# Second up phase of a decoder step: another order of five products, an earlier load, one copy replaced

## The chip, the cores and the metric

The kernel runs on one core of a Trainium2 chip. The metric is device time in microseconds, the median of three runs. TensorE (PE) multiplies; VectorE (DVE) and ScalarE (ACT) prepare its weights and read its results out of PSUM; SyncE (SP) issues nearly all loads and stores; GpSimd (POOL) does little.

## The reference

One layer of a decoder serves a prompt of 512 tokens and 8 samples of 4 tokens, 544 columns in all, in float32. It consists of a combined input projection, a pooling mixer, a sparse attention, an output projection, and a ConvFFN. The change lies in the ConvFFN:

```python
up = rmsnorm(h, g_pre_ffn) @ w_up            # 2048 -> 2 x 5632
val, gate = jnp.split(up, 2, axis=-1)
gcat = jnp.concatenate([conv_hist, gate], axis=1)
conv = conv_b
for j in range(CONV_WIDTH):                  # three taps along the tokens
    conv = conv + conv_w[j] * gcat[:, j:j + T]
y = (jax.nn.gelu(conv, approximate=True) * val) @ w_down
h = h + rmsnorm(y, g_post_ffn)
```

## The kernel before

**Layout.** Activations lie with channels on the 128 partitions and the 544 tokens in two halves of 272 (H2). Every product of float32 numbers is made of three matmuls: high part by high part, low part of the activations by high part of the weights, and high by low (lines 354, 355 and 356). So each block of weights is split first: ScalarE casts it to its high part (wh, line 232), and VectorE subtracts that to get the low part (wl, line 234). `Weights` walks through a list of units that `plan()` writes; a unit here is 8 blocks of 128x128, 512 KB, multiplied with 272 columns in 24 matmuls. While one unit is multiplied, the unit two places further is split (line 254, with `ahead` 2): its cast is issued after the first of 8 blocks, its low part after the sixth. Before a unit begins, `get()` runs the functions that were hooked to its number (line 248).

**The up projection in two phases.** It is done for 44 column tiles j (FT) in a scheme of the Strassen-Winograd kind on 2x2 blocks: half the channels by half the tokens on one side, the value and gate tiles by half the channels on the other. The first phase multiplies with the plain first half of the tokens and leaves in `stash_d`, in DRAM, 128x544 numbers for each j: in one half a partial sum, in the other the finished gate with its activation. The second phase, which the change touches, runs one group for each j with five products, whose activations are the prepared forms t2, t1, t3, t4 and b22. Their weights are four sums of quarters of `w_up` and one plain quarter (3):

- s1 = q2 + q3, s2 = s1 - q0, s3 = q0 - q2, s4 = q1 - s2, each a 128x1024 operation on VectorE (line 1338). `give()` hooks the loads of the quarters (line 206, called by `quarter`) and these sums to units before the one that uses them.

**One group.** A group has two PSUM banks, `ug` (`pa`) and `utr` (`ph`), each with two buffers that take turns between groups. An identity matmul first puts the stash's first half (`sl`) into ug (line 1487); then t2 is added to ug, t1 starts utr, t3 is added to ug, t4 to ug, and b22 to utr. In between the results are read: u2 is ug after t2 (ScalarE, line 1489), u3 is ug after t3 (ScalarE, line 1492), val is u3 + utr after t1 (VectorE, line 1493), act is the stash's second half times ug after t4 (line 1495), and ge, the gate, is u2 + utr after b22 (lines 1500 and 1501). `conv()` then hangs the three taps, the GELU and the product with val on a clock that ticks with the blocks of the units (`later`). act and val go to `act_d` in DRAM (lines 1496 and 1443), from where the down phase loads them.

**What sets the order.** All engines work in program order, and the program is the order in which this code is written. SP's queue is in that order too: a load that waits holds up those behind it. `prefetch(j + 1)` loads the next stash (line 1415) and copies two edges into the next ge; before the change it stands behind the store of act.

Of the kernel before, what the change touches and what calls it, by code (L numbers as in the profile page):

```python
# [12 lines left out]
F32 = mybir.dt.float32  # L13
# [3 lines left out]
OP = mybir.AluOpType  # L17
# [4 lines left out]
P = 128  # L22
# [5 lines left out]
TOK = SEQ + NB * NS  # L28
H2 = TOK // 2
# [5 lines left out]
FT = DFF // P  # L35
# [16 lines left out]
def kinner(mat, m, kts=None, halves=BOTH):  # L52
    kts = list(range(KT) if kts is None else kts)
    return [(tuple((mat, k, m) for k in kts[i:i + 8]), halves) for i in range(0, len(kts), 8)]


def kouter(mat, ms):
    return [(tuple((mat, k + i, m) for i in range(2) for m in ms), BOTH) for k in range(0, KT, 2)]


def grp(gs):
    return [(tuple(("grp%d" % g, k, m) for g in gs for m in range(2) for k in range(2)), BOTH)]


def plan():
    u = kouter("in", [0, 1, 2])
    for m in range(3, 21):
        u += kinner("in", m)
    for m in GATES[:30]:
        u += kinner("in", m)  # L70
    for m in range(8):
        u += kinner("in", M_POOL + m)
        if m == 6:
            u += grp((0, 1))
    for m in GATES[30:]:
        u += kinner("in", m)
    u += grp((2, 3))
    for m in range(KT + 1):
        if m < KT:
            u += kinner("pp", m, range(8))  # L80
        if m:
            u += kinner("np", m - 1, range(8))
    for m in range(KT - NSPLIT):
        u += kinner("out", m)
    for h in BOTH:
        for m in range(KT - NSPLIT, KT):
            u += kinner("out", m, halves=(h,))
    for j in range(0, FT, 2):
        u += [(quad(i, q), (0,)) for q in (0, 1) for i in (j, j + 1)]
    for j in range(FT):  # L90
        u += [(quad(j, q), (0,)) for q in ("s2", "s1", "s3", 3, "s4")]
    for a, b in CHUNKS:
        if b - a == 8:
            for m in range(KT):
                u += kinner("dn", m, range(a, b))
        else:
            for hs in (BOTH,) if b < FT else ((0,), (1,)):
                for m in range(0, KT, 2):
                    u += [(tuple(("dn", k, m + i) for i in range(2) for k in range(a, b)), hs)]
    return u  # L100


def quad(j, q):


    if isinstance(q, str):
        return tuple((q, k, j) for k in range(KH))
    return tuple(("up", q % 2 * KH + k, (FT if q < 2 else 0) + j) for k in range(KH))
# [159 lines left out]
def layer(ctx: ExitStack, tc: tile.TileContext, a: dict):  # L268
    nc = tc.nc
    ctx.enter_context(tc.manual_schedule())  # L270
    ctx.enter_context(nc.allow_non_contiguous_dma(reason="short rows of the token states"))
    V, S, G, T = nc.vector, nc.scalar, nc.gpsimd, nc.tensor
# [17 lines left out]
    ws = Weights(nc, wp, a["wst"], plan())  # L290
# [12 lines left out]
    act_d = dr.tile([FT, P, TOK], F32, name="act_d")  # L303

    HS = (slice(0, H2), slice(H2, TOK))
# [27 lines left out]
    def later(n, fn):  # L333
        deferred.append([n, fn])
# [987 lines left out]
    raws, ffn = {}, {}  # L1322
# [9 lines left out]
    def quarter(j, q, bufs=1):  # L1332
        t = raws[j, q] = ffn["fw"].tile([P, 1024], F32, name=f"wq{q}_{j}", tag=f"q{q}", bufs=bufs)
        ws.fetch(t, quad(j, q))

    def weight_sum(j, n, x, y, op):
        t = raws[j, n] = ffn["fw"].tile([P, 1024], F32, name=f"w{n}_{j}", tag="sum", bufs=3)
        V.tensor_tensor(t, raws[j, x], raws[j, y], op)  # L1338

    def hook(i, f):  # L1340
        ws.hooks.setdefault(i, []).append(f)

    def give(j, b):


        def fetch():
            quarter(j, 2)
            quarter(j, 0)

        def fetch_last():  # L1350
            quarter(j, 3, 2)
            ws.raw[b + 3] = raws[j, 3]

        def s1():
            weight_sum(j, "s1", 2, 3, OP.add)
            ws.raw[b + 1] = raws[j, "s1"]

        def s2():
            weight_sum(j, "s2", "s1", 0, OP.subtract)
            ws.raw[b] = raws[j, "s2"]  # L1360
            quarter(j, 1)

        def s3():
            weight_sum(j, "s3", 0, 2, OP.subtract)
            ws.raw[b + 2] = raws[j, "s3"]

        def s4():
            weight_sum(j, "s4", 1, "s2", OP.subtract)
            ws.raw[b + 4] = raws[j, "s4"]

        for x, f in ((-6, fetch_last), (-5, fetch), (-3, s1), (-2, s2), (-1, s3), (1, s4)):
            hook(b + x, f)
        ws.given.update(range(b, b + 5))

# [21 lines left out]
    for j in range(0, FT, 2):  # L1396
        pa = [psp.tile([P, 512], F32, name=f"p1_{i}", tag=t, bufs=2)[:, :H2] for i, t in ((j, "g"), (j + 1, "tr"))]
        st = {}
# [10 lines left out]
    GE = 2 + SEQ - H2 + NB * 6  # L1409
    gw, gw_es = pool("gate", "right")  # L1410
    ge, stash = {}, {}

    def prefetch(j):
        stash[j] = cp.tile([P, TOK], F32, name=f"sl{j}", tag="gz", bufs=2)
        nc.sync.dma_start(stash[j], stash_d[j])
        g = ge[j] = gw.tile([P, GE], F32, name=f"ge{j}", tag="ge", bufs=2)
        S.copy(g[:, 0:2], edge[:, j, :])
        S.copy(g[:, 2 + SEQ - H2:].rearrange("p (b k) -> p b k", k=6)[:, :, 0:2], ch[:, j])

    def conv(j, val):  # L1420

        g = ge.pop(j)
        o = SEQ - H2
        gs = g[:, 2 + o:].rearrange("p (b k) -> p b k", k=6)
        c = gw.tile([P, GE], F32, name=f"cv{j}", tag="cv", bufs=2)
        n = GE - 2

        def first():
            S.activation(c[:, :n], g[:, :n], AF.Identity, bias=cw[:, j, 3:4], scale=cw[:, j, 0:1])
            S.copy(co[:, j, 0:2], g[:, o:o + 2])  # L1430
            S.copy(co[:, j, 2:].rearrange("p (b k) -> p b k", k=2), gs[:, :, 4:6])

        def rest():
            V.scalar_tensor_tensor(c[:, :n], g[:, 1:n + 1], cw[:, j, 1:2], c[:, :n], OP.mult, OP.add)
            V.scalar_tensor_tensor(c[:, :n], g[:, 2:n + 2], cw[:, j, 2:3], c[:, :n], OP.mult, OP.add)
            S.activation(c[:, :n], c[:, :n], AF.Gelu_apprx_tanh)

        def last():
            V.tensor_tensor(val[:, :o], val[:, :o], c[:, :o], OP.mult)
            V.tensor_tensor(val[:, o:].rearrange("p (b k) -> p b k", k=4),  # L1440
                            val[:, o:].rearrange("p (b k) -> p b k", k=4),
                            c[:, 2 + o:].rearrange("p (b k) -> p b k", k=6)[:, :, 0:4], OP.mult)
            nc.sync.dma_start(act_d[j][:, HS[1]], val)

        later(0.4, first)
        later(1.6, rest)
        later(4.6, last)
# [21 lines left out]
    def preps(c0, c1, pl_, tag, n):  # L1469
        for j in range(c0, c1):  # L1470
            yield from act_prep(j, pl_, tag, n)

    prefetch(0)
    for j in range(FT):
        pa, ph = [psp.tile([P, 512], F32, name=f"u{t}{j}", tag=t, bufs=2)[:, :H2] for t in ("g", "tr")]

        def product(ps, form, start):
            xh, xl = forms[form]
            unit(lambda *_: [ps], lambda mat, k, h: (xh[:, k % KH, :], xl[:, k % KH, :]),
                 lambda k: start and k % KH == 0, lambda k: k % KH == KH - 1, skip=True)  # L1480

        st, g = stash.pop(j), ge[j]
        u = gw.tile([P, TOK], F32, name=f"us{j}", tag="us", bufs=2)
        u2, u3 = u[:, HS[0]], u[:, HS[1]]
        val = gw.tile([P, H2], F32, name=f"val{j}", tag="val", bufs=2)
        a1 = gw.tile([P, H2], F32, name=f"act{j}", tag="act", bufs=2)
        T.matmul(pa, ident, st[:, HS[0]], start=True, stop=False, skip_group_check=True)
        product(pa, "t2", False)
        S.copy(u2, pa)
        product(ph, "t1", True)  # L1490
        product(pa, "t3", False)
        S.copy(u3, pa)
        V.tensor_tensor(val, u3, ph, OP.add)
        product(pa, "t4", False)
        V.tensor_tensor(a1, st[:, HS[1]], pa, OP.mult)
        nc.sync.dma_start(act_d[j][:, HS[0]], a1)
        if j + 1 < FT:
            prefetch(j + 1)
        product(ph, "b22", False)
        V.tensor_tensor(g[:, 2:2 + SEQ - H2], u2[:, :SEQ - H2], ph[:, :SEQ - H2], OP.add)  # L1500
        V.tensor_tensor(g[:, 2 + SEQ - H2:].rearrange("p (b k) -> p b k", k=6)[:, :, 2:6],
                        u2[:, SEQ - H2:].rearrange("p (b k) -> p b k", k=4),
                        ph[:, SEQ - H2:].rearrange("p (b k) -> p b k", k=4), OP.add)
        conv(j, val)
        if j == FT - 4:
            bg["gen"], bg["rate"], bg["credit"] = preps(*CHUNKS[0], ap0, "a0", 2), 0.3, 1.0
    drain()
# [196 lines left out]
```

## Time and profile before

| | before |
|---|---|
| median of 3 runs | 3074.69 us (3072.78 to 3075.41) |
| profiled execution | 3077.14 us, its span 3075.5 us |
| PE busy | 2916.3 us (95%) |
| PEld (weight loads) busy | 2808.7 us (91%) |
| DVE busy | 1789.6 us (58%) |
| ACT busy | 1118.6 us (36%) |
| POOL busy | 259.7 us (8%) |
| HBM traffic | 139 GB/s over the span |

The table is from the page's first and third part. PE's busy time is a sum over pipelined matmuls whose ends are modelled, so the time that it really needs is read from the distances between starts. The second up phase lies between 1714 and 2512 us of the span.

### The profile page before, as it was taken

The numbers are of one execution on the slowest core, as the hardware profiler recorded it, in microseconds if no ns is written. First come the engines' busy times: TensorE is split into PE (matmuls) and PEld (weight loads), VectorE is DVE, ScalarE is ACT, GpSimd is POOL, SyncE is SP. The second block draws the span as 40 slices with busy tenths as digits, with TensorE's granted clock in tenths as the row PEclk, the third lists the DMA queues.
The fourth block names the chain that finished last, engine by engine and source line by source line (L and its number), as shares of the span: only waits on it lengthen the run. The fifth ranks groups of instructions, "written<-read, shape, count | busy, mean of one in ns | idle before, by whom it ended". The sixth has DMA issues, their size and how long they took to land.

```text
span 3075.5 us, 56483 instructions
## 1 busy us (share of the span) xinstructions
PE 2916.3 (95%) x22887; PEld 2808.7 (91%) x22887; DVE 1789.6 (58%) x3189; ACT 1118.6 (36%) x2227; POOL 259.7 (8%) x356
## 2 busy tenths in 40 slices
PE   9799999999999999998999889888988899999996
PEld 9698888999999999998999888888888899999996
DVE  7232435777755544358785677777777763444347
ACT  4111224444432322245665344344434443222223
POOL 4232220000003000122100000000000000000004
PEclk9899999999999999999999999999999999999998
DMA  6542564122225443256766444444444453333234
GB/s 207 134 136 94 200 224 149 63 74 77 77 73 99 138 133 126 88 169 196 249 220 228 147 154 155 143 139 156 156 140 139 150 173 112 115 112 105 100 104 151
DMA packets 185283, 431.02 MB, mean 140 GB/s; under 512 B 39611, under 2 KB 77916, under 8 KB 185022
## 3 DMA queue, kind: packets, MB, share of 16 engines
q1 hardware_dynamic: 161240, 395.94, 38.8%
q10 hardware_dynamic: 16614, 14.68, 2.2%
q0 software_dynamic: 7168, 16.79, 1.8%
q8 instruction: 179, 2.93, 0.4%
q14 instruction: 82, 0.67, 0.1%
HBM read 369.23 MB, written 58.11 MB: 139 GB/s over the span
## 4 chain that ended last, share of the span: by engine, by line
PE 80%; DVE 7%; DMA 6%; issue 3%; ACT 3%; SPq 1%; POOL 0%; DVEq 0%; ACTq 0%; POOLq 0%
PE in L354 7%; PE in L356 6%; PE in L355 6%; PE dn L356 5%; PE dn L355 5%; PE dn L354 5%; DMA sl<-stash_d 4%; PE ug L354 3%; PE ug L356 3%; PE ug L355 3%; PE p L356 2%; PE p L354 2%; PE p L355 2%; DVE ws L1338 2%; ACT wh L232 2%
## 5 line engine op out<-in xcount | busy, mean ns | idle before, releaser
L232 ACT CAST wh<-wr 128x512 fp32r<-128x512 f32 (+2 forms) x636 | 425.3, 697 | 786.3 <-PE dn L355 329.6
L234 DVE TENSOR_TENSOR wl<-wr,wh 128x512 fp32r<-128x512 f32 (+2 forms) x636 | 516.2, 817 | 299.9 <-ACT wh L232 292.1
L354 PE MATMUL in<-uh,wh 128*128 128x272 f32 x1600 | 490.3, 306 | 0.0
L356 PE MATMUL in<-uh,wl 128*128 128x272 f32 x1600 | 462.4, 289 | 0.0
L355 PE MATMUL in<-ul,wh 128*128 128x272 f32 x1600 | 461.3, 288 | 0.0
L356 PE MATMUL dn<-h,wl 128*128 128x272 f32 x1312 | 379.7, 289 | 0.0
L354 PE MATMUL dn<-h,wh 128*128 128x272 f32 x1312 | 378.0, 288 | 0.1
L355 PE MATMUL dn<-l,wh 128*128 128x272 f32 x1312 | 377.2, 287 | 0.0
L354 PEld LDWEIGHTS in<-uh,wh 128*128 128x128 f32 x1600 | 302.0, 189 | 39.0 <-issue 37.9
L355 PEld LDWEIGHTS in<-ul,wh 128*128 128x128 f32 x1600 | 303.1, 189 | 0.7
L356 PEld LDWEIGHTS in<-uh,wl 128*128 128x128 f32 x1600 | 301.7, 189 | 0.0
L232 ACT CAST wh<-ws 128x1024 fp32r<-128x1024 f32 x176 | 184.5, 1048 | 242.9 <-PE utr L355 89.2
L234 DVE TENSOR_TENSOR wl<-ws,wh 128x1024 fp32r<-128x1024 f32 x176 | 215.0, 1222 | 66.7 <-ACT wh L232 66.7
L355 PEld LDWEIGHTS dn<-l,wh 128*128 128x128 f32 x1312 | 247.3, 188 | 0.0
L354 PEld LDWEIGHTS dn<-h,wh 128*128 128x128 f32 x1312 | 247.0, 188 | 0.3 <-issue 0.2
L356 PEld LDWEIGHTS dn<-h,wl 128*128 128x128 f32 x1312 | 246.6, 188 | 0.0
L1562 DVE TENSOR_TENSOR y<-y,dn 128x272 f32<-128x272 f32 x160 | 70.0, 437 | 248.0 <-PE dn L356 248.0
L354 PE MATMUL p<-vh,wh 128*128 128x272 f32 x704 | 204.8, 291 | 4.3 <-ACT st L1404 4.3
L356 PE MATMUL p<-vh,wl 128*128 128x272 f32 x704 | 204.1, 290 | 1.4 <-DVE wl L234 1.4
L355 PE MATMUL p<-vl,wh 128*128 128x272 f32 x704 | 202.7, 288 | 0.0
L356 PE MATMUL wo<-mh,wl 128*128 128x272 f32 x512 | 150.9, 295 | 15.9 <-DVE wl L234 15.9
L1592 POOL TENSOR_TENSOR accf<-accf,sqf 128x272 f32<-128x272 f32 x26 | 21.4, 822 | 1541.0 <-ACT sqf L1590 1540.9
(362 smaller groups left out, 7458.2 us busy)
## 6 DMA issues: line engine op xcount, KB each, us to landing
wr<-wst SPq DMA_DIRECT2D x376, 512.0 KB, 3.5
wq<-wst SPq DMA_DIRECT2D x176, 512.0 KB, 4.8
stash_d<-st SPq DMA_DIRECT2D x44, 272.0 KB, 2.2
sl<-stash_d SPq DMA_DIRECT2D x44, 272.0 KB, 2.9
ar<-act_d SPq DMA_DIRECT2D x44, 272.0 KB, 3.0
sg_d<-gz SPq DMA_DIRECT2D x32, 272.0 KB, 2.2
X<-cache POOLq DMA_DIRECT2D x128, 64.0 KB, 2.8
act_d<-act SPq DMA_DIRECT2D x44, 136.0 KB, 1.7
```

What stands on the lines that cost most here:

```text
L232: self.nc.scalar.copy(hi[:, c], raw[:, c])
L234: self.nc.vector.tensor_tensor(lo[:, c], raw[:, c], hi.bitcast(F32)[:, c], OP.subtract)
L354: T.matmul(ps, wh, xh, start=first(k), stop=False, skip_group_check=skip)
L355: T.matmul(ps, wh, xl, start=False, stop=False, skip_group_check=skip)
L356: T.matmul(ps, wl, xh, start=False, stop=last(k), skip_group_check=skip)
L1338: V.tensor_tensor(t, raws[j, x], raws[j, y], op)
L1562: V.tensor_tensor(y[:, m, HS[h]], y[:, m, HS[h]], pss[m][h], OP.add)
L1592: G.tensor_tensor(accf[:, HS[h]], accf[:, HS[h]], q, OP.add)
```

## The change

Five edits, all in the second up phase:

- The products of a group come in the order t2, t1, t3, b22, t4 instead of t2, t1, t3, t4, b22, so the units of the plan and the numbers under which `give()` hands over the sums change places. s4 is made at the start of the group's first unit instead of its second.
- The load of quarter 1 is hooked one unit earlier.
- `prefetch(j + 1)` stands at the beginning of group j instead of near its end, and ge gets a third buffer.
- ScalarE no longer copies ug after t3 (u3). It copies utr after t1 into val, and VectorE adds ug after t3 to val.
- act and its store move behind t4, which is now the group's last product.

```diff
@@ plan()
-        u += [(quad(j, q), (0,)) for q in ("s2", "s1", "s3", 3, "s4")]
+        u += [(quad(j, q), (0,)) for q in ("s2", "s1", "s3", "s4", 3)]
@@ give(j, b)
         def fetch_last():
             quarter(j, 3, 2)
-            ws.raw[b + 3] = raws[j, 3]
+            ws.raw[b + 4] = raws[j, 3]
 
         def s1():
+            quarter(j, 1)
             weight_sum(j, "s1", 2, 3, OP.add)
             ws.raw[b + 1] = raws[j, "s1"]
 
         def s2():
             weight_sum(j, "s2", "s1", 0, OP.subtract)
             ws.raw[b] = raws[j, "s2"]
-            quarter(j, 1)
...
             weight_sum(j, "s4", 1, "s2", OP.subtract)
-            ws.raw[b + 4] = raws[j, "s4"]
-
-        for x, f in ((-6, fetch_last), (-5, fetch), (-3, s1), (-2, s2), (-1, s3), (1, s4)):
+            ws.raw[b + 3] = raws[j, "s4"]
+
+        for x, f in ((-6, fetch_last), (-5, fetch), (-3, s1), (-2, s2), (-1, s3), (0, s4)):
             hook(b + x, f)
@@ prefetch(j)
-        g = ge[j] = gw.tile([P, GE], F32, name=f"ge{j}", tag="ge", bufs=2)
+        g = ge[j] = gw.tile([P, GE], F32, name=f"ge{j}", tag="ge", bufs=3)
@@ the group
-        u = gw.tile([P, TOK], F32, name=f"us{j}", tag="us", bufs=2)
-        u2, u3 = u[:, HS[0]], u[:, HS[1]]
+        u2 = gw.tile([P, H2], F32, name=f"us{j}", tag="us", bufs=2)
...
+        if j + 1 < FT:
+            prefetch(j + 1)
         T.matmul(pa, ident, st[:, HS[0]], start=True, stop=False, skip_group_check=True)
         product(pa, "t2", False)
         S.copy(u2, pa)
         product(ph, "t1", True)
+        S.copy(val, ph)
         product(pa, "t3", False)
-        S.copy(u3, pa)
-        V.tensor_tensor(val, u3, ph, OP.add)
-        product(pa, "t4", False)
-        V.tensor_tensor(a1, st[:, HS[1]], pa, OP.mult)
-        nc.sync.dma_start(act_d[j][:, HS[0]], a1)
-        if j + 1 < FT:
-            prefetch(j + 1)
+        V.tensor_tensor(val, val, pa, OP.add)
         product(ph, "b22", False)
...
         conv(j, val)
+        product(pa, "t4", False)
+        V.tensor_tensor(a1, st[:, HS[1]], pa, OP.mult)
+        nc.sync.dma_start(act_d[j][:, HS[0]], a1)
```

The next rows are VectorE's order in group 21, before, from the add into val to the low part of s3. `ws1_22` to `ws3_22` are the sums of the next group, `wl` are low parts, and the source in the middle of a `wl` row names the weights.

```order
L1493 TENSOR_TENSOR val21_24546<-us21_24545,utr21_24544 128x272
L1338 TENSOR_TENSOR ws2_22_24653<-ws1_22_24621,wq0_22_24551 128x1024
L234 TENSOR_TENSOR wl404_24661<-ws2_22_24653,wh404_24660 128x1024
L1495 TENSOR_TENSOR act21_24547<-sl21_24503,ug21_24543 128x272
L1338 TENSOR_TENSOR ws3_22_24692<-wq0_22_24551,wq2_22_24549 128x1024
L234 TENSOR_TENSOR wl405_24700<-ws1_22_24621,wh405_24699 128x1024
L1500 TENSOR_TENSOR ge21_24505<-us21_24545,utr21_24544 128x240
L1501 TENSOR_TENSOR ge21_24505<-us21_24545,utr21_24544 128x8x4
L1434 SCALAR_TENSOR_TENSOR cv21_24726<-ge21_24505,cw_17346,cv21_24726 128x288
L1435 SCALAR_TENSOR_TENSOR cv21_24726<-ge21_24505,cw_17346,cv21_24726 128x288
L234 TENSOR_TENSOR wl406_24741<-ws3_22_24692,wh406_24740 128x1024
```

The same stretch in the changed kernel:

```order
L1494 TENSOR_TENSOR val21_24552<-val21_24552,ug21_24549 128x272
L1338 TENSOR_TENSOR ws2_22_24660<-ws1_22_24629,wq0_22_24564 128x1024
L234 TENSOR_TENSOR wl404_24666<-ws2_22_24660,wh404_24665 128x1024
L1496 TENSOR_TENSOR ge21_24372<-us21_24551,utr21_24550 128x240
L1497 TENSOR_TENSOR ge21_24372<-us21_24551,utr21_24550 128x8x4
L1338 TENSOR_TENSOR ws3_22_24693<-wq0_22_24564,wq2_22_24562 128x1024
L1434 SCALAR_TENSOR_TENSOR cv21_24692<-ge21_24372,cw_17346,cv21_24692 128x288
L1435 SCALAR_TENSOR_TENSOR cv21_24692<-ge21_24372,cw_17346,cv21_24692 128x288
L234 TENSOR_TENSOR wl405_24701<-ws1_22_24629,wh405_24700 128x1024
L1502 TENSOR_TENSOR act21_24553<-sl21_24370,ug21_24549 128x272
L1338 TENSOR_TENSOR ws4_22_24744<-wq1_22_24627,ws2_22_24660 128x1024
```

The rows of ge and the conv steps have moved ahead of act, and act, which stood right behind the low part of s2, now stands behind that of s1.

SP's queue, before, from one store of act to the next (`wq3_22` is quarter 3 of group 22):

```order
L1496 DMA act_d_81<-act20_24363 128x272
L1415 DMA sl21_24503<-stash_d_80 128x544
L206 DMA wq3_22_24510<-wst 128x1024
L206 DMA wq2_22_24549<-wst 128x1024
L206 DMA wq0_22_24551<-wst 128x1024
L1443 DMA act_d_81<-val20_24362 128x272
L206 DMA wq1_22_24655<-wst 128x1024
L1496 DMA act_d_81<-act21_24547 128x272
```

And in the changed kernel:

```order
L1503 DMA act_d_81<-act20_24369 128x272
L1415 DMA sl22_24554<-stash_d_80 128x544
L206 DMA wq2_22_24562<-wst 128x1024
L206 DMA wq0_22_24564<-wst 128x1024
L1443 DMA act_d_81<-val20_24368 128x272
L206 DMA wq1_22_24627<-wst 128x1024
L206 DMA wq3_23_24695<-wst 128x1024
L1503 DMA act_d_81<-act21_24553 128x272
```

Behind the store of act20 now goes the stash of group 22 instead of 21, and quarter 3 has moved from ahead of quarter 2 to the end of the row, ahead of the next store of act.

## Rows read from the trace of the kernel before

**Rows 1.** TensorE's waits in the second up phase: total us, times, longest us.
```profile
PE ug L1487 <- DMA sl<-stash_d: 66.1, 44, 6.1
PE ug L354 <- ACT us L1492: 20.9, 44, 0.5
```

**Rows 2.** Timeline, TensorE: start, us, engine, line, operation, out<-in, shapes, [idle before].
```profile
2103.80 0.29 PE L354 MATMUL ug<-t3h,wh 128*128 128x272 f32 x1
...
2106.70 0.29 PE L356 MATMUL ug<-t3h,wl 128*128 128x272 f32 x1
...
2107.46 0.39 PE L354 MATMUL ug<-t4h,wh 128*128 128x272 f32 x1 [0.47 <-ACT us L1492]
...
2107.69 0.29 PE L355 MATMUL ug<-t4l,wh 128*128 128x272 f32 x1
...
2113.49 0.29 PE L356 MATMUL utr<-b22h,wl 128*128 128x272 f32 x1
...
2115.08 0.73 PE L1487 MATMUL ug<-sl,misc 128*128 128x272 f32 x2 [1.30 <-DMA sl<-stash_d]
...
2115.77 0.29 PE L355 MATMUL ug<-t2l,wh 128*128 128x272 f32 x1
```

**Rows 3.** The chain that ended last, one group: start, us, what.
```profile
2097.19 0.73 PE ug L1487 x2
...
2107.02 0.40 ACT us L1492
...
2107.80 1.23 DVE ws L1338
2109.10 1.06 ACT wh L232
...
2111.33 0.44 DVE act L1495
...
2112.21 2.83 DMA sl<-stash_d
```

**Rows 4.** Windows: length, busy PE, PEld, DVE, ACT, POOL; clock, DMA share, GB/s.
```profile
1800.00:2000.00 200.00, 178.85 (x1343) 173.18 (x1342) 144.55 (x187) 80.49 (x144) 0.00 (x0) 0.99 0.44 147
2369.00:2371.00 2.00, 2.00 (x11) 2.00 (x10) 1.38 (x3) 0.00 (x0) 0.00 (x0) 0.50 0.74 297
2520.00:2620.00 100.00, 100.00 (x797) 100.00 (x797) 40.53 (x68) 38.34 (x81) 0.00 (x0) 1.00 0.40 131
```

**Rows 5.** Timeline, VectorE and SP in the group of rows 2.
```profile
2107.44 0.44 DVE L1493 TENSOR_TENSOR val<-us,utr 128x272 f32<-128x272 f32 x1 [1.22 <-ACT us L1492]
...
2110.18 1.23 DVE L234 TENSOR_TENSOR wl<-ws,wh 128x1024 fp32r<-128x1024 f32 x1 [1.17 <-ACT wh L232]
...
2112.68 1.35 SPq L206 DMA_DIRECT2D wq<-wst  x3
...
2113.95 0.39 DVE L1500 TENSOR_TENSOR ge<-us,utr 128x240 f32<-128x240 f32 x1
2114.26 0.18 DVE L1501 TENSOR_TENSOR ge<-us,utr 128x32 f32<-128x32 f32 x1
...
2115.34 0.52 DVE L1434 SCALAR_TENSOR_TENSOR cv<-ge,cw,cv 128x288 f32<-128x288 f32 x1 [0.91 <-ACT cv L1429]
```

**Rows 6.** Transfers issued from 2112.4 to 2113.0: count, KB each, us to landing.
```profile
wq<-wst SPq DMA_DIRECT2D x1, 512.0 KB, 3.7
```

**Rows 7.** Timeline, TensorE, a group in which the clock falls.
```profile
2366.92 0.73 PE L1487 MATMUL ug<-sl,misc 128*128 128x272 f32 x2 [1.87 <-DMA sl<-stash_d]
...
2372.00 0.29 PE L354 MATMUL utr<-t1h,wh 128*128 128x272 f32 x1
```

**Rows 8.** Timeline, TensorE, first matmuls of the phase and of the down phase.
```profile
1714.12 1.27 PE L1487 MATMUL ug<-sl,misc 128*128 128x272 f32 x2 [6.10 <-DMA sl<-stash_d]
...
2512.28 0.29 PE L354 MATMUL dn<-h,wh 128*128 128x272 f32 x1
```

**Rows 9.** Instructions of line 1489: ns min/median/max, first and last start.
```profile
L1489 ACT COPY us<-ug x44: 386/387/391, 1720.2 to 2499.6; 128x272 f32<-128x272 f32 x44
```

**Rows 10.** Loads of line 206 from 1800 to 2400: time to landing.
```profile
DMA to landing us min/median/max: 3.5/4.9/6.8
```

## The prediction

> **What bounds the kernel now.** I read the waits of TensorE first, over the second up phase alone. Only two kinds stand there: the first matmul of a group waits for the load of its stash, and the first matmul of the product t4 waits for ScalarE's copy of the bank that it adds to; both come 44 times, once in each group [rows 1]. Next the timeline of one group, for what a wait costs in time of the engine, since a busy or idle sum of pipelined matmuls does not give it. In t3 the last of 24 matmuls starts 2.90 us after the first, so matmuls start every 0.126 us and a product takes 3.03 us [rows 2]. Between t3's last start and t4's first there are 0.76 us, so 0.63 are lost, and the one after it comes 0.23 us later, so another 0.10 is lost to refilling. From b22's last start to the identity matmul there are 1.59 us: 1.46 lost [rows 2]. The period of the group is 2115.08 - 2097.19 = 17.89 us [rows 3].
>
> The chain of waits says why the stash is late. Its load is ready to go long before, but it is issued behind the store of act, and act is the last in a line: sum s2, cast of s2, its low part, act, then the store and the load, 2.83 us until it lands [rows 3]. So the wait is not one for bandwidth; the load is asked for too late.
>
> Last the other engines: in 200 us of the phase VectorE is busy 144.55 and ScalarE 80.49 [rows 4], which per group of 17.89 us is 12.9 and 7.2. Neither bounds; but VectorE works in program order, and a group without waits leaves it less room.
>
> **The change part by part.** *Removed: the wait for the stash.* The load now goes out a whole group earlier (sl22 stands right behind act20 on SP's queue, not sl21). It leaves some 0.9 us after act's start and lands 2.83 us later [rows 3], about 5 us after the start of the group before the one that needs it, ten microseconds early. The load itself, two ScalarE copies of ge's edges and their third buffer cost nothing on the path: ScalarE is under half busy.
>
> *Removed: the wait of t4.* The order is now t2, t1, t3, b22, t4 in banks a, h, a, h, a, and the next group's a is another buffer. Each read of a bank has a whole product, 3.03 us, between the matmul that ends it and the next that adds to it. The copy of t2's result and the new copy of t1's result (the same 128x272 as before, 0.40 us) start 0.32 us after a product's last matmul starts [rows 2, 3]; the add into val comes at the same distance after t3 and takes 0.36 to 0.44 us. All are done 2 us before the bank is wanted. The copy of t3's result is gone and that of t1's takes its place, so ScalarE's sum stays.
>
> *What is left for TensorE in a group:* five products, 5 x 24 x 0.126 = 15.13 us, and the identity matmul. After a wait it costs 2115.77 - 2115.08 - 0.126 = 0.56 us; without one, by what t4's refill showed, 0.46. I take 0.52 and a period of **15.65 us**.
>
> *What is late next.* I set t = 0 at the start of t2, let products start at 0, 3.03, 6.05, 9.08 and 12.10, and put VectorE's work in its new order with the spacings of one group [rows 5]: 1.15 us from one 1024-wide operation to the next, s2 to its cast 1.30 [rows 3], cast to low part 1.08. Low part of s4 from 4.6; s1 of the next group from 6.4 (when its quarter lands, below); low part of q3 7.6 to 8.75, wanted by t4 at 12.1; val at 9.3; s2 9.65, its cast 10.95, its low part 12.0 to 13.2, wanted at 15.65; ge 13.2; s3 13.7; the two conv steps 14.85; low part of s1 15.9 to 17.05, wanted at 18.7; act 17.05; s4 17.4; the val products; low part of s3 19.15 to 20.3, wanted at 21.7; then the low part of s4 at 20.3, which is 4.65 in the next group: it closes on itself. The smallest margin is 1.4 us, so TensorE does not wait.
>
> *The loads.* Each group still issues seven transfers. The load of quarter 3 now stands ahead of act's store and waits for the low part of q3 (8.75); behind it on SP are only act's store at 17.05, the stash and the loads of q2 and q0, so it holds nobody up. q1 is loaded one product earlier than it was and is wanted at 17.4. q2 and q0 move up a place, to third and fourth of the burst that act's store opens. That makes a loop: act, store, stash, q2, s1, ..., low part of s1, act. Before the change, the third of these transfers is issued at 2112.68 and takes 3.7 us [rows 5, 6], so it lands 5.05 us after act starts. VectorE's part is 1.15 (s1) + 1.15 (low q3) + 0.36 (val) + 1.30 + 1.08 + 1.15 (s2, cast, low part) + 0.49 (ge) + 1.15 (s3) + 1.04 (conv) + 1.15 (low s1) = 10.0. The loop takes 15.1 us, 0.6 less than TensorE's 15.65. It is the closest thing to a new limit.
>
> *The clock.* In the phase the granted clock falls in four groups after the first, each time after a stash wait longer than usual. At 2366.92 the wait was 1.87 us; then the clock was 0.50 of full, the lower of its two levels (1.2 and 2.4 GHz) [rows 4, 7], and the next product began 5.08 us after the identity matmul, against 0.56 + 3.03 = 3.59: 1.5 us lost. With the waits the four falls should go, 6 us in all. The Trainium skill speaks against the new order here: its page "TensorE: Matmul & The Clock Gate", section "A second HAM failure mode: psum-queue depth-cycling", says that cycling through PSUM banks makes TensorE idle briefly and lets its clock swing between the two levels. No row here bears that out: the down phase, which also goes from bank to bank between products, is at 1.00 [rows 4].
>
> *The sum.* The phase runs from 1714.12 to the first down matmul at 2512.28 [rows 8]: 798.2 us, 18.14 per group (17.89, the four slow groups, and a first group that starts at the low clock: its first copy comes 6.08 us after the identity matmul instead of 0.56 + 3.03 + 0.2 [rows 8, 9], 2.3 us more). The first group's own stash wait stays, since that load is where it was. After: 44 x 15.65 + 2.3 = 690.9. Saved: 107.3 us. The work before and after the phase is untouched; the down phase starts without a wait today, and the last group's conv now begins a product earlier. The profiled execution took 3077.14 us (span 3075.5), 2.45 above the median of the runs; taken off the median 3074.69 the saving gives 2967.4. I add half a microsecond for odd waits: **2968 us**.
>
> **The rivals.**
> *VectorE becomes the bound.* 12.9 us of work per group, plus the 1.1 us it must stand while ScalarE casts s2, plus its waits for t3 (0.5) and for the cast of q3 (up to 0.7), come to 15.2 of 15.65: against it is that margin, for it that it is small and that VectorE cannot reorder. If it is 1 us per group worse than that sum says, the saving shrinks by some 25 us: 2993; by 2 us: 3035.
> *The load loop sets the pace; the slower side.* Landings of quarters range from 3.5 to 6.8 us, with a median of 4.9 [rows 10], where my loop uses 3.7. With 4.9 the loop is 16.3 and the time 44 x 0.6 = 26 us more, 2994; with 6.8 it is 18.2, as long as today's 18.14, no change. From there on every microsecond costs 44: at 8 us, with loads crowding in a phase that now moves the same bytes in less time, 3074 + 44 x 1.2 = 3127. Against it: the median mixes first and last of three transfers, and quarter 3 no longer goes ahead of q2. The point from which it decides is 5.6 us from act to q2's landing; slower begins at 8.1.
> *The stash wait is only renamed.* If the identity matmul finds another reason to wait, only t4's 0.73 us go: 44 x 0.73 = 32, 3043. Against it: its only other needs are a free bank, read a group earlier.
> *The clock swings with the banks.* One fall per group at 1.5 us takes 66 us back: 3034. What the rows on the clock show speaks against it. (This is the time that the Trainium skill's rule on cycling banks would give.)
>
> **How the numbers follow.** The forecast, TensorE back to back to within 0.5 us a group: 0.85, 2961 (identity at 0.46, no odd waits, a few microseconds of clock) to 2990. VectorE or the loop at a partial loss: 0.07, 2990 to 3035. Stash wait renamed: 0.015. Clock: 0.015. No change, the loop at today's pace: 0.02. Slower, the loop beyond 18.14: 0.03. Faster by over 0.2% (6 us, about what a measurement here can tell from no change) is 0.85 + 0.07 + 0.03 = 0.95, same 0.02, slower 0.03. The range 2960 to 2993 leaves out the cases above 2993.
>
> **What would show it.** Right: the second up phase takes about 690 us, the period is 15.6 to 15.7, no wait of the identity matmul but the first, none of t4, granted clock 1.00 throughout after the first group, VectorE busy over 80% of the phase. Wrong: matmuls of t2, t1 or t3 waiting for a low part (VectorE bounds), or VectorE's sum s1 waiting for a load of wq (the loop).

## The result

The changed kernel takes 2973.98 us (median of 4 runs, 2971.68 to 2976.06), the one before beside it 3075.05 (3072.78 to 3076.14): a ratio of 0.9672, with a 95% interval of 0.9655 to 0.9689. The forecast was 2968. The profiled execution took 2971.68, with a span of 2970.0 against 3075.5.

TensorE's waits in the second up phase of the changed kernel, in the columns of [rows 1]: us in total, times, longest.

```profile
PE ug L1488 <- DMA sl<-stash_d: 5.9, 1, 5.9
PE utr L354 <- ACT val L1492: 1.9, 1, 1.9
PE utr L356 <- DVE wl L234: 0.5, 1, 0.5
```

The identity matmul waits once, in the first group, where [rows 1] had 44 waits, and t4 never. Two rows of the chain that ended last give the period, 2028.37 - 2012.78 = 15.59 us, where [rows 3] had 17.89:

```profile
2012.78 0.46 PE ug L1488 x2
...
2028.37 0.46 PE ug L1488 x2
```

The same 200 us as the first of [rows 4], with the same columns: TensorE is busy throughout, the granted clock is 1.00, and VectorE has risen from 144.55 to 166.01, which is 83%.

```profile
1800.00:2000.00 200.00, 200.00 (x1567) 198.98 (x1566) 166.01 (x219) 91.46 (x167) 0.00 (x0) 1.00 0.50 172
```

The phase lasts from the first identity matmul to the first down matmul, as in [rows 8]: 692.7 us, where it was 798.2.

```profile
1714.26 1.28 PE L1488 MATMUL ug<-sl,misc 128*128 128x272 f32 x2 [5.88 <-DMA sl<-stash_d]
...
2406.93 0.29 PE L354 MATMUL dn<-h,wh 128*128 128x272 f32 x1
```

So the profiled spans differ by 105.5 us and the phase by the same; what lies before and after it takes as long as it did.

### The profile page after: what moved, and what is told of

Same layout as the page of the kernel before. It is cut to its first block, busy times and chain, and to the rows that moved or that the text cites. A ratio compares the mean times of both kernels' runs of the same rounds, so it can differ in the third digit from the quotient of the medians.

```text
span 2970.0 us, 56562 instructions
## 1 busy us (share of the span) xinstructions
PE 2891.0 (97%) x22887; PEld 2800.6 (94%) x22887; DVE 1781.1 (60%) x3189; ACT 1112.8 (37%) x2227; POOL 259.7 (9%) x356
## 3 DMA queue, kind: packets, MB, share of 16 engines
q0 software_dynamic: 7168, 16.79, 1.8%
q8 instruction: 179, 2.93, 0.4%
## 4 chain that ended last, share of the span: by engine, by line
PE 87%; DVE 6%; DMA 3%; issue 2%; ACT 2%; SPq 0%; POOL 0%; ACTq 0%; DVEq 0%; POOLq 0%
PE in L354 7%; PE in L356 7%; PE in L355 7%; PE dn L356 6%; PE dn L355 5%; PE dn L354 5%; PE ug L354 4%; PE ug L356 4%; PE ug L355 4%; PE p L354 3%; PE p L356 3%; PE p L355 3%; PE utr L356 2%; PE utr L354 2%; PE utr L355 2%; PE wo L356 2%
## 5 line engine op out<-in xcount | busy, mean ns | idle before, releaser
L356 PE MATMUL wo<-mh,wl 128*128 128x272 f32 x512 | 151.0, 295 | 15.7 <-DVE wl L234 15.6
L354 PE MATMUL wo<-mh,wh 128*128 128x272 f32 x512 | 149.6, 292 | 0.0
```

The source lines that it names most:

```text
L354: T.matmul(ps, wh, xh, start=first(k), stop=False, skip_group_check=skip)
L356: T.matmul(ps, wl, xh, start=False, stop=last(k), skip_group_check=skip)
```

## The experiments

The theory: two waits of TensorE, of 1.56 and 0.73 us a group, add up, and with both gone TensorE is back to back. What limits next is a loop through VectorE and SP (act, store, loads, sum s1, ..., low part of s1, act), only a little shorter than TensorE's group. The rivals: one of the waits hides the other; the order of the products alone does it; VectorE's total sets the pace. Of the five edits, the earlier load of quarter 1, the earlier s4 and the third buffer of ge were not tried alone.

**One part alone: the early load.** The kernel before, with prefetch at the start of the group.

```diff
-        g = ge[j] = gw.tile([P, GE], F32, name=f"ge{j}", tag="ge", bufs=2)
+        g = ge[j] = gw.tile([P, GE], F32, name=f"ge{j}", tag="ge", bufs=3)
...
+        if j + 1 < FT:
+            prefetch(j + 1)
         T.matmul(pa, ident, st[:, HS[0]], start=True, stop=False, skip_group_check=True)
...
-        if j + 1 < FT:
-            prefetch(j + 1)
```

> The kernel before, with one part of the change: the stash is loaded a group ahead (and ge has a third buffer); order of the products and copies stay. My theory, two waits that add: the stash wait goes (1.46 us a group and the falls of the clock), t4's wait stays (0.73 us a group), so the period is 15.59 + 0.73 = 16.3 us and the time 2974 + 44 x 0.73 = 3006 us. Rival, the early load only uncovers VectorE's lateness: the identity matmul stops waiting and matmuls of t2 wait for low parts instead, time near 3075.

Measured: 3002.27 us (ratio 0.9768, 0.9751 to 0.9784). Its TensorE waits:

```profile
PE ug L354 <- ACT us L1494: 20.9, 44, 0.5
PE ug L1489 <- DMA sl<-stash_d: 5.6, 1, 5.6
```

The stash wait is gone, that of t4 stands at the very 20.9 us of [rows 1], and the clock is at 1.00 in every stretch of 20 us after the first. Its period is 16.33 us:

```profile
2012.48 0.46 PE ug L1489 x2
2028.81 0.46 PE ug L1489 x2
```

That is 0.74 more than in the changed kernel, the price of t4's wait in the prediction. By the medians the rest of the change is worth 3002 - 2974 = 28 us, 0.65 a group; the changed kernel loses some of it again in other waits (below). The waits add.

**One part undone: the load behind act.**

```diff
-        if j + 1 < FT:
-            prefetch(j + 1)
         T.matmul(pa, ident, st[:, HS[0]], start=True, stop=False, skip_group_check=True)
...
         nc.sync.dma_start(act_d[j][:, HS[0]], a1)
+        if j + 1 < FT:
+            prefetch(j + 1)
```

> The changed kernel with one part undone: the stash of the next group is loaded behind the store of act again, and act is now the last product's. My theory, the place in SP's queue behind act is what makes the stash late: act, 0.9 us to the issue, 2.83 us to landing, 0.5 identity, 15.1 of products, 0.2 to the next act: a period of 19.6 us, 3150 us, and up to 3216 if the clock falls in every group (1.5 us each). Rival, the order of the products is what counts and the load would be in time from either place: 2974.

Measured: 3324.42 us (1.082, 1.0802 to 1.0838), 8% slower than before the change; the direction was right, the size was not. The chain of this kernel, a group:

```profile
2112.68 1.22 DVE wl L234
2113.90 0.36 DVE act L1500
2114.28 0.33 SPq L1501
2114.70 2.81 DMA sl<-stash_d
2117.55 1.27 PE ug L1486 x2
...
2141.57 1.27 PE ug L1486 x2
```

The period is 24.02 us, not 19.6. Issue and landing took 3.65 us from act's start, as expected. But TensorE waits 5.3 us before the first of these identity matmuls and 5.5 before the second, so act starts some 1.7 us after the products end: VectorE is still at the conv steps and the low part of s1, which stand ahead of act in its new order. And the mean granted clock is 0.86:

```profile
1800.00:2000.00 200.00, 151.74 (x995) 147.68 (x995) 110.64 (x145) 59.61 (x111) 0.00 (x0) 0.86 0.33 114
```

From one identity matmul to the end of the products this leaves 24.0 - 5.5 = 18.5 us where 15.6 are needed at full clock: 2.9 us a group are lost to the low clock, twice what one fall cost in [rows 7]. (In this group the clock was at 0.50 for the first 5.9 us.) So the reordering without the early load is a loss: the two parts of the change are not independent in that direction.

**How early must the load be?**

```diff
-        if j + 1 < FT:
-            prefetch(j + 1)
         T.matmul(pa, ident, st[:, HS[0]], start=True, stop=False, skip_group_check=True)
...
         conv(j, val)
+        if j + 1 < FT:
+            prefetch(j + 1)
         product(pa, "t4", False)
```

> The changed kernel with the load of the next stash issued just before the last product, so only about a product and a half ahead, but ahead of act's store. My theory, it only has to stand ahead of act: it is issued soon after quarter 1 and lands 7 us before the identity matmul; 2974 us, within 5. Rival, a whole group of lead is needed: the identity matmul waits, 1 us a group or more, 3018 or more.

Measured: 2968.44 us (0.9663, 0.9647 to 0.9679), so this place ahead of act's store is early enough. It is no test of a short lead, though. SP runs ahead of TensorE, and in the trace the load goes out 11.0 us before the identity matmul that reads it (median), against 12.5 in the changed kernel; how late it could go stays open. The time was even 5.5 us less than the changed kernel's, so both were run again side by side:

> The changed kernel again, on the same chip as the next two, for comparison: 2971 to 2977 us.

> The load of the next stash just before t4 again, beside the changed kernel on the same chip. Theory: 2 to 6 us less than the changed kernel, because TensorE's wait in group 41 (2.4 us by the profile) is gone; rival: the 5.5 us between the first two results are the spread of the runs, and both take 2970 to 2975.

Measured: 2973.20 us (2971.07 to 2975.12) and 2967.37 (2966.02 to 2970.89): 5.8 us, and the ranges do not meet. In the profile of the first run the stash is out of the burst of loads that follows act's store, quarter 2 stands directly behind that store, VectorE waits for loads 22.4 us instead of 53.9, and TensorE's waits are one:

```profile
PE ug L1486 <- DMA sl<-stash_d: 6.3, 1, 6.3
```

In the profiles the phase is 4.7 us shorter. Group 41 (below) takes 2.2 us less; the rest lies mainly in groups 24 to 29, where the loop sets the changed kernel's pace (see the point on slack below), and in the last group.

**The old way of val, in the new order.**

```diff
-        u2 = gw.tile([P, H2], F32, name=f"us{j}", tag="us", bufs=2)
+        u = gw.tile([P, TOK], F32, name=f"us{j}", tag="us", bufs=2)
+        u2, u3 = u[:, HS[0]], u[:, HS[1]]
...
-        S.copy(val, ph)
         product(pa, "t3", False)
-        V.tensor_tensor(val, val, pa, OP.add)
+        S.copy(u3, pa)
+        V.tensor_tensor(val, u3, ph, OP.add)
```

> The changed kernel with the old way of val: ScalarE copies ug after t3, VectorE adds that and utr, and then b22 may add to utr. So the order of the products is new and the read before b22 is two steps behind t3. My theory, the read must have a product's time: b22 waits for copy and add, 0.32 + 0.40 + 0.44 us and the refill against a spacing of 0.13, about 1.2 us a group, 3027 us. Rival, the new order alone is enough: 2974.

Measured: 3024.35 us (0.9838, 0.9822 to 0.9855). b22 waits in each of 44 groups:

```profile
PE utr L354 <- DVE val L1495: 44.8, 44, 3.8
...
2102.45 0.46 PE ug L1489 x2
2119.24 0.46 PE ug L1489 x2
```

The first row is from its waits, the other two from its chain: a period of 16.79, 1.20 more than 15.59, as worked out. The order alone does not do it: a bank read at the last moment costs that much. How much less than a whole product's time would do was not tried.

**The loop: quarter 2 one transfer later.**

```diff
         def fetch():
-            quarter(j, 2)
             quarter(j, 0)
+            quarter(j, 2)
```

> The changed kernel with the loads of quarters 2 and 0 in the other order, so that quarter 2, which the sum s1 waits for, lands one 512 KB transfer (about 1.35 us) later. Loop theory: in the changed kernel the loop act, store, loads, s1, ..., act is only 0.1 to 0.2 us shorter than TensorE's 15.59; it becomes 16.8 and sets the pace: 2974 + 44 x 1.2 = 3027 us. Rival, VectorE has idle time to absorb it: 2974.

Measured: 3054.77 us (0.995, 0.9934 to 0.9965): nearly the whole gain is lost by the order of two loads. The chain of this kernel is the loop itself:

```profile
2120.38 0.36 DVE act L1502
2120.76 0.33 SPq L1503
2121.18 0.38 SPq L1415
2121.65 1.73 SPq L206
2123.43 0.43 SPq L206
...
2130.45 0.35 DVE val L1494
2130.80 1.15 DVE ws L1338
2132.05 1.06 ACT wh L232
...
2136.80 1.22 DVE wl L234
2138.02 0.36 DVE act L1502
```

Its period is 2138.02 - 2120.38 = 17.64 us, 2.05 more than TensorE needs, not 1.2. The part from s1 to act is as before, 9.84 us in the median of 37 groups in both traces; what grew is the part from act to s1, from 5.77 to 7.69. The issue of the first quarter, 1.73 us in these rows, is not the reason: its median is 0.40, and only three of 36 took over 1 us, as two did in the changed kernel. In the median quarter 2 is issued 0.46 us later behind act, since one more load goes out before it, and s1 starts 5.87 us after that issue, where it was 4.30. I had counted one transfer at 1.35 us and left out the issue. In four groups the clock also fell, and these took 2 us and more above the median. So the loop is shown, but my price for it was about half.

**The same with the stash out of the burst.** The kernel with the load just before t4, and the two loads exchanged in the same way.

> Quarter 2 loaded last of the two, as in the run with quarters exchanged, but with the stash out of that burst (loaded just before t4). Loop theory: quarter 2 stands third behind act again, as in the changed kernel, but behind 512 KB of weights instead of 272 KB of stash; the period is 15.6 plus 0.6 (0.5 to 0.8 us more landing, less the 0.15 of slack), 2995 to 3005 us. Rival, it is only the exchange of the quarters (a longer issue on SP) that costs: as slow as that run, 3045 to 3055.

Measured: 2993.43 us (0.9749, 0.9734 to 0.9763), a little under the range of the theory and some 50 under the rival's. The median period is 16.02 us. The exchange by itself does not cost what it cost with the stash ahead.

**The loop: a spare operation on it, and off it.** One VectorE subtraction of 912 columns a group into a spare tile, either right before act or right behind the products with val.

```diff
+        def spare():
+            d = gw.tile([P, 4, 228], F32, name=f"spare{j}", tag="spare", bufs=1)
+            x, y = [forms[n][0].bitcast(F32)[:, 0:4, 0:228] for n in ("t1", "t2")]
+            V.tensor_tensor(d, x, y, OP.subtract)
...
+        spare()
         V.tensor_tensor(a1, st[:, HS[1]], pa, OP.mult)
```

> The changed kernel with one spare VectorE subtraction of 912 columns (about 1.03 us) a group, right before act, which lies on the loop. Loop theory: period 15.59 + 1.03 - 0.15 = 16.5, 3013 us. Rival, VectorE's total sets the pace: this kernel and the one with the same operation behind the products with val take the same time.

> The changed kernel with the same spare VectorE operation a group, but behind the products with val, off the loop, where VectorE then stands waiting for quarter 2 for about 1 us. Loop theory: no change, 2974 to 2980 us. Rival, VectorE's total sets the pace: as long as with the operation ahead of act, 3013 in both, or no loss in either.

Measured: 3013.95 us (0.9811, 0.9796 to 0.9826) on the loop, 2974.38 (0.9687, 0.9672 to 0.9701) off it. The same work costs 40 us in one place and nothing in the other, so VectorE's total does not set the pace. VectorE's waits for loads, first on the loop and then off it:

```profile
DVE ws L1338 <- DMA wq<-wst: 53.3, 42, 2.9
```

```profile
DVE ws L1338 <- DMA wq<-wst: 14.5, 26, 1.3
```

Off the loop the operation fills the time in which VectorE stood waiting for quarter 2.

**A version that beats both.** Two stalls are left in the changed kernel. One is the first group's wait for the stash, with the low clock after it. The other is in group 41, here in its rows of SP, ScalarE and TensorE:

```profile
2362.70 0.43 SPq L1460 DMA_DIRECT2D ar<-act_d  x1
...
2367.88 0.64 ACT L1464 CAST h<-ar 128x544 fp32r<-128x544 f32 x1 [5.59 <-DMA ar<-act_d]
2368.43 0.38 ACT L1492 COPY val<-utr 128x272 f32<-128x272 f32 x1
...
2368.87 0.39 PE L354 MATMUL utr<-b22h,wh 128*128 128x272 f32 x1 [1.90 <-ACT val L1492]
```

ScalarE waits 5.59 us for a load of the down phase's activations, and behind it stands the copy into val, and behind that b22. The new version loads the half of the first stash that the identity matmul reads into a tile of its own while the first phase still runs, and starts the loads of `ar` two groups earlier, with two more steps between load and cast.

```diff
+    sl0 = fs.tile([P, H2], F32, name="sl0")
...
+        if j == FT - 6:
+            nc.sync.dma_start(sl0, stash_d[0][:, HS[0]])
...
-        T.matmul(pa, ident, st[:, HS[0]], start=True, stop=False, skip_group_check=True)
+        T.matmul(pa, ident, st[:, HS[0]] if j else sl0, start=True, stop=False, skip_group_check=True)
...
-        if j == FT - 4:
-            bg["gen"], bg["rate"], bg["credit"] = preps(*CHUNKS[0], ap0, "a0", 2), 0.3, 1.0
+        if j == FT - 6:
+            bg["gen"], bg["rate"], bg["credit"] = preps(*CHUNKS[0], ap0, "a0", 2, 4), 0.3, 1.0
```

> The changed kernel with its two leftover stalls removed: the half of the first stash that the identity matmul reads is loaded before the first up phase ends, into a tile of its own, and the first loads of the down phase's activations start two groups earlier and land before ScalarE is asked to cast them. My theory: the first group's wait (5.9 us) and its stretch at the low clock (2.3 us) go, and the 2.1 us that TensorE waits in group 41, so 2974 - 10 = 2964 us. Rival, another wait takes the first one's place (the first group's low parts or sums): 2970 to 2972.

Measured: 2963.48 us (0.9655, 0.9642 to 0.9668). The stretch around the phase's start, in the changed kernel and in this one, busy as in [rows 4]:

```profile
1700.00:1720.00 20.00, 14.12 (x94) 13.66 (x93) 10.35 (x12) 7.06 (x16) 0.00 (x0) 0.83 0.54 188
```

```profile
1700.00:1720.00 20.00, 20.00 (x159) 19.92 (x158) 14.64 (x16) 9.03 (x19) 0.00 (x0) 1.00 0.52 184
```

TensorE goes through without a gap and at full clock. Last, the same with the stash loaded just before t4:

> The kernel with both leftover stalls removed, and besides the load of the next stash just before the last product instead of at the group's start. Theory: the loop's slack grows (quarter 2 lands 0.8 us sooner after act) but TensorE is already back to back, so nothing more is gained: 2960 to 2965 us, as before this step. Rival: the earlier landing also takes away waits that the profile of one execution misses, 2957 or less.

Measured: **2960.11 us** (2959.17 to 2961.34; 0.9636, 0.9623 to 0.9649), the best of all, with no wait of TensorE in the list of the phase. The two versions ran on different chips, but the traces show the same difference: the phase takes 689.7 us without that step and 686.2 with it. Without it six groups took 16.0 to 16.8 us, and TensorE waited 0.9 us for val and 0.9 for low parts; with it two groups were above 15.6. So the step does gain, as the rival said, and the theory that nothing was left to gain was wrong.

## Why the prediction was right, point by point

- *The stash is late because it stands behind act, not for want of bandwidth.* Shown from both sides: moved ahead of act alone, it saves 71 us; put back behind act, which by then is the last product's, it costs 350, low clock included.
- *A period of 15.65 us.* Measured 15.59: the identity matmul without a wait costs the 0.46 that the refill after t4 had suggested. 44 x 0.06 = 2.6 us in the kernel's favour.
- *t4's wait, 0.73 us a group.* With the early load alone the period is 0.74 longer than with the whole change, and 1.20 longer, as expected, when a read stands two steps behind.
- *The order of VectorE closes on itself.* It does: the low part of q3, worked out for 7.6 to 8.75 after t2's start, starts in the changed kernel at 7.8; s1, expected at 6.4, at 6.7.
- *The loop has 0.6 us of slack.* This term was mis-sized: there is next to none. These are VectorE's rows in one group:

```profile
2014.34 0.43 DVE L1502 TENSOR_TENSOR act<-sl,ug 128x272 f32<-128x272 f32 x1
...
2019.92 1.23 DVE L1338 TENSOR_TENSOR ws<-wq,wq 128x1024 f32<-128x1024 f32 x1 [1.03 <-DMA wq<-wst]
2021.06 1.22 DVE L234 TENSOR_TENSOR wl<-wq,wh 128x1024 fp32r<-128x1024 f32 x1
2022.36 0.44 DVE L1494 TENSOR_TENSOR val<-val,ug 128x272 f32<-128x272 f32 x1
...
2029.93 0.43 DVE L1502 TENSOR_TENSOR act<-sl,ug 128x272 f32<-128x272 f32 x1
```

  From s1 to act they take 10.0 us, to the tenth what was worked out, 0.15 of it in waiting for TensorE between the starts of q3's low part and of val (1.30 against 1.15). From act to s1 they take 5.58, where 5.05 was taken from before. Over 37 groups in the middle of the phase the medians are 9.84 and 5.77, together 15.61, against TensorE's 15.59. The prediction put the point from which the loop decides at 5.6 us from act to q2's landing, and s1, which waits for it, starts there. One of its signs of being wrong did appear: s1 waits for a load of wq in 42 groups, 57.0 us in all. In groups 24 to 29, where act to s1 took 5.8 to 6.7 us, the loop did set the pace: the period was 15.7 to 16.0, 1.7 us lost in all, and the chain that ended last runs through the loads:

```profile
2077.99 0.36 DVE act L1502
...
2079.25 5.29 DMA wq<-wst
...
2094.56 0.36 DVE act L1502
...
2095.83 4.41 DMA wq<-wst
```

  Why so little was lost: the low part of s1, which ends as act starts, can be late without TensorE waiting. Act starts 1.72 us after the identity matmul at the earliest and up to 2.93 in the groups before these; it is at 3.5 to 3.9 in those where t1 starts or goes on late. That the loop came out at TensorE's own pace is luck; the sum did not show it. The four runs on the loop (40 us for 1 us of work, 81 for one load later, 19 with the stash out of the way, none off it) agree. The rival had 0.05 for the old pace or worse and a part of the 0.07 for a partial loss: it was the near miss.
- *The clock.* After the first group every stretch of 16 us is at 1.00; the falls went with the waits. The group now changes its bank at every product, and that did nothing to the clock. The Trainium skill, page "TensorE: Matmul & The Clock Gate", section "A second HAM failure mode: psum-queue depth-cycling", tells of a kernel where cycling through banks made TensorE idle briefly and the clock swing; this trace shows no swing after the first group.
- *The sum.* 107.3 us expected, 105.5 between the profiled spans, 101.1 between the medians; the profiled execution before lay above its median and the one after below. What I had not seen is the wait in group 41: the wait for `ar` that ScalarE had in the kernel before, 0.4 us, grew to 5.6 when the same instructions met another order on SP, and took b22 with it. In the profile it costs 2.2 us, about what the shorter identity matmul gives. The loop costs 1.7 us in groups 24 to 29, and the last group takes 0.7 more, where t1 waits 0.5 us for a low part.

## What to carry to other kernels

When a transfer that is ready is late, look at what stands ahead of it in its queue before looking at its size: here the whole gain of the load lies in standing ahead of one store. Leave time between the matmul whose result is read from a bank and the next that adds to it: here a whole product between them cost nothing, and a copy and an add put in at the last moment cost their length and more. And after such a change close the next loop by hand, transfers and their issue included, and over many groups, not one: an engine at 83% had room for 1 us of work in one place and for about 0.1 in another.

## What was not expected of the hardware

A longer wait costs more than its length: with some 5.4 us of waiting in each group the granted clock falls every time, and the products take 18.5 us instead of 15.6. In the kernel before, where TensorE stood idle 1.1 to 2.2 us ahead of each identity matmul after the first, the clock fell in four groups of 43, after 1.80, 2.18, 1.87 and 1.86 us; another 1.86 went by without a fall. The issue of one 512 KB load on SP took 0.33 to 0.45 us in nearly all cases and 1.1 to 2.0 us now and then, in up to four of some 140 in a run, the kernel before and the changed one among them; no run here shows why.
